# Windowed attention in a hybrid encoder layer: keys and values of a key head split once for all tokens, scaling by the sum on VectorE, two query buffers

## The chip, the core and the metric

The kernel runs on one core of a Trainium2 chip. The core has a matrix engine (TensorE, "PE" in the profile, with its weight loads shown apart as "PEld"), a vector engine (VectorE, "DVE"), a scalar engine (ScalarE, "ACT"), GpSimd ("POOL"), and SyncE ("SP"), which issues nearly all transfers of this kernel. Each engine works through its own queue of instructions in order and waits on semaphores for the others. The metric is device time in microseconds (us); lower is better.

## What is computed

One layer of an encoder for 1024 tokens of width 1024, in float32. It has four parts with RMS norms around them: a mixer with two branches that run side by side, (A) windowed attention and (B) a gated DeltaNet in both directions; one output projection of both; cross-attention into 256 memory tokens; and a SwiGLU feed-forward layer. The change touches branch (A). Eight query heads of width 64 share two key heads, four each, and a block of 128 queries sees its own block of keys and the two beside it. A learned "sink" logit takes part in the sum of the softmax. Cut to this branch:

```python
def _window_attention(q, k, v, sink):
    ...
    kw, vw = band(k), band(v)
    scores = jnp.einsum('bnqhgd,bnkhd->bnhgqk', qb, kw) * (ATTN_HEAD_DIM ** -0.5)
    ...
    scores = jnp.where(mask[None, :, None, None], scores, -jnp.inf)
    sk = sink.astype(jnp.float32).reshape(ATTN_KV_HEADS, ATTN_GROUP)[None, None, :, :, None, None]
    m = jnp.maximum(jnp.max(scores, axis=-1, keepdims=True), sk)
    p = jnp.exp(scores - m)
    denom = jnp.sum(p, axis=-1, keepdims=True) + jnp.exp(sk - m)
    o = jnp.einsum('bnhgqk,bnkhd->bnqhgd', p / denom, vw)
    return o.reshape(b, s, ATTN_WIDTH)
```

## The kernel before

Matrix products of float32 data are done on operands split in two: a high part, which is the value rounded to the type float32r by a copy on ScalarE, and a low part, which is the value less the high part, by a subtraction on VectorE or GpSimd. Three products (high by high, high by low, low by high) are added in PSUM. The helper `split` (lines 99 to 106) does this, and `load_w` (118 to 129) loads a slab of weights of 512 KB into one of two `wraw` buffers and splits it into `whi` and `wlo`.

The mixer is written as three lists of steps, which `issue` (687 to 690) runs in order. `ORDER_1` has the projections and preparation of the DeltaNet (`D`, `P`, `B`). `ORDER_2`, "G0 G1 G2 G3 L0 L1 V A4 A0 A1 W L2 L3 W W A2 A3 W", has the gate projections (`G`), the later levels of the DeltaNet's block inverses (`L`), the projections of values (`V`), keys (`A4`) and queries (`A0` to `A3`), and calls of `next_windows` (`W`). `ORDER_3` begins with `M`, the norm of the memory tokens, then five times "s01 W K", then further `s01` and `K`, and eight `K` at its end. `s01` is one of eight steps of the DeltaNet's scan for both head groups, a recurrence of small matrix products (line 763) with VectorE and ScalarE steps between them. `K` (`next_kv`, 883 to 902) is one of sixteen projections of the memory tokens for the cross-attention: 24 matmuls (891), a copy on ScalarE (893), a transfer, and for the last eight a transpose and a second copy (899, 901).

The program is put in order when it is built: a scheduler takes the instructions of each engine by priority, in general the order in which they are written, but puts a later one ahead where it is ready sooner by its own estimate. So windows, scan steps and projections are interleaved on every engine, and what stands later in the lists can run earlier.

Queries, keys and values go through DRAM: `attn_proj` (701 to 716) writes rotated queries and keys to `d_q` and `d_k` (head dimension by tokens), `value_proj` (718 to 729) writes `d_v` (token blocks by token by head dimension).

A window is one block of 128 queries with one key head: 8 blocks by 2 key heads, 16 windows. `window(n, g)` (598 to 666) is a generator in two halves. The first loads keys of the two or three blocks in sight twice, to both halves of the partitions (610), the block's queries of four heads likewise (611), and values (613). Keys and values are split here, for this window alone: `khi` on ScalarE (616), `klo` on GpSimd (617), `vhi` (621) and `vlo` (622), values doubled so that the product puts each head on both halves of the partitions. Queries hold the high part on partitions 0 to 63 and the low part on 64 to 127 (624, 625), so one matmul with 128 rows adds both. The raw keys, queries and values have one buffer each. Scores of a head are two matmuls (633) into a bank `pw` of PSUM; VectorE adds the band mask, scales, and takes the maximum (635); ScalarE takes the exponential with its sum (642); the sink's term comes in on four columns (645 to 647), the reciprocal on VectorE (648), and ScalarE multiplies each head's row by it (650). After the `yield` come, for each block of keys, four transposes into a `pw` bank (656), its split (659: cast on ScalarE, subtraction on VectorE) and three matmuls with the values as weights into `pow` (661). Two copies (664, 665) bring the even and the odd heads to the two halves of the partitions, and a transfer (666) writes them to `d_mix`.

`next_windows` (668 to 677) starts two windows a call and lets the second half of each window come after the first half of the next. After the scan, `d_mix` is read back (1023) and split, the output projection runs (`mid_gemm`, 967 to 1006), and the memory keys and values are read back and split (1033 to 1036).

Of the kernel before, what the change touches and what calls it, by code (L numbers as in the profile page):

```python
# [10 lines left out]
F32 = mybir.dt.float32  # L11
F32R = mybir.dt.float32r
I32 = mybir.dt.int32
AF = mybir.ActivationFunctionType
ALU = mybir.AluOpType
# [4 lines left out]
P = 128  # L20
S = 1024
D = 1024
KT = D // P
NT = S // P
HALF = 512
# [50 lines left out]
def tile_hybrid_block(  # L76
# [6 lines left out]
    nc = tc.nc  # L83
# [9 lines left out]
    def f32(ap):  # L93
        return ap.bitcast(F32)

    def bc(ap, axis, shape):
        return ap.unsqueeze(axis).to_broadcast(list(shape))
# [10 lines left out]
    def pool(name, bufs, **kw):  # L108
        return tc.tile_pool(name=name, bufs=bufs, reuse_waits="tile", **kw)
# [64 lines left out]
    d_k = dram.tile([P, S], F32, name="d_k")  # L174
    d_v = dram.tile([NT, P, P], F32, name="d_v")
# [346 lines left out]
    def levels(h):  # L522
# [72 lines left out]

        together([part(b) for b in range(2)])

    def window(n, g):

        tok = slice(n * P, (n + 1) * P)  # L600
# [1 line left out]
        nb = k1 - k0  # L602
        w = nb * P
        band = C[:, _AT["band0"] - C0 + (k0 - n + 1) * P:][:, 0:w]


        kr = tw.tile([P, 384], F32, tag="kr", name="kr", bufs=1)[:, 0:w]
        qr = tw.tile([P, 4, P], F32, tag="qr", name="qr", bufs=1)
        for r in range(2):
            nc.sync.dma_start(kr[64 * r:64 * r + 64], d_k[64 * g:64 * g + 64, k0 * P:k1 * P])  # L610
            nc.sync.dma_start(qr[64 * r:64 * r + 64], d_q[256 * g:256 * g + 256, tok].rearrange("(h e) t -> e h t", h=4))
        vr = tw.tile([P, 3, 64], F32, tag="vr", name="vr", bufs=1)[:, 0:nb]
        nc.sync.dma_start(vr, d_v[k0:k1, :, 64 * g:64 * g + 64].rearrange("c p e -> p c e"))
        khi = tw.tile([P, 384], F32R, tag="khi", name="khi")[:, 0:w]
        klo = tw.tile([P, 384], F32R, tag="klo", name="klo", bufs=1)[:, 0:w]
        nc.scalar.copy(khi, kr)
        nc.gpsimd.tensor_tensor(klo, kr, f32(khi), ALU.subtract)
        vhi = tw.tile([P, 3, 2, 64], F32R, tag="vhi", name="vhi")[:, 0:nb]
        vlo = tw.tile([P, 3, 2, 64], F32R, tag="vlo", name="vlo")[:, 0:nb]
        v2 = bc(vr, 2, (P, nb, 2, 64))  # L620
        nc.scalar.copy(vhi, v2)
        nc.gpsimd.tensor_tensor(vlo, v2, f32(vhi), ALU.subtract)
        qs = tw.tile([P, 4, P], F32R, tag="qs", name="qs")
        nc.scalar.copy(qs, qr)
        nc.gpsimd.tensor_tensor(qs[64:128], qr[64:128], f32(qs[64:128]), ALU.subtract)
# [4 lines left out]
        for hh in range(4):  # L630
            pp = pw.tile([P, 512], F32, tag="pw", name="psw")
            for i, kk in enumerate((khi, klo)):
                nc.tensor.matmul(pp[:, 0:w], qs[:, hh, :], kk, start=(i == 0), stop=(i == 1))
            sc = tw.tile([P, 384], F32, tag="sc", name="sc", bufs=8)
            nc.vector.tensor_tensor_reduce(out=sc[:, 0:w], in0=pp[:, 0:w], in1=band, scale=0.125,
                                           scalar=sink[:, 4 * g + hh:4 * g + hh + 1], op0=ALU.add, op1=ALU.max,
                                           accum_out=m4[:, hh:hh + 1])
            pr.append(sc)
# [8 lines left out]
        nc.vector.tensor_tensor(es, es, ssum, ALU.add)  # L647
        nc.vector.reciprocal(es, es)
        for hh in range(4):
            nc.scalar.mul(pr[hh][:, 0:w], pr[hh][:, 0:w], es[:, hh:hh + 1])  # L650
        yield
        po = pw.tile([P, 4, P], F32, tag="pow", name="pow", bufs=1)
        for j in range(nb):
            pp = pw.tile([P, 512], F32, tag="pw", name="ptw")
            for hh in range(4):
                nc.tensor.transpose(pp[:, hh * P:(hh + 1) * P], pr[hh][:, j * P:(j + 1) * P], ident)
            ph = tw.tile([P, 512], F32R, tag="ph", name="ph")
            pl = tw.tile([P, 512], F32R, tag="pl", name="pl")
            split(ph, pl, pp)
            for i, (vv, pe_) in enumerate(((vhi, ph), (vhi, pl), (vlo, ph))):  # L660
                nc.tensor.matmul(po.rearrange("p h t -> p (h t)"), vv[:, j].rearrange("p r e -> p (r e)"), pe_,
                                 start=(j == 0 and i == 0), stop=(j == nb - 1 and i == 2))
        ao = tw.tile([P, 2, P], F32, tag="ao", name="ao", bufs=1)
        nc.scalar.copy(ao[0:64], po[0:64, 0:4:2, :])
        nc.scalar.copy(ao[64:128], po[64:128, 1:4:2, :])
        nc.sync.dma_start(d_mix[g * 256:(g + 1) * 256, tok].rearrange("(k p) t -> p k t", p=P), ao)

    def next_windows():

        for _ in range(2):  # L670
            last = wins[-1] if wins else None
            if wins_done[0] < 2 * NT:
                wins.append(window(wins_done[0] % NT, wins_done[0] // NT))
                next(wins[-1])
            wins_done[0] += 1
            if last:
                next(last, None)

    wins, wins_done = [], [0]
    kqv = {0: kqv0}  # L680
# [15 lines left out]
    pw = p12.enter_context(pool("pw", 2, space=PSUM, side="right"))  # L696
    ps = pgs.enter_context(pool("psl", 2, space=PSUM))
    tw = p12.enter_context(pool("tw", 2))
    tl_ = p1.enter_context(pool("tl", 2))

    def attn_proj(ct):
# [669 lines left out]
```

## Time and profile before

| what | value |
|---|---|
| median of 3 runs | 1644.9 us (1640.13 to 1646.33) |
| the profiled execution: time, span | 1638.65 us, 1636.9 us |
| mean granted TensorE clock | 0.984 |
| ACT: scaling of rows, line 650 | 64 instructions, 32.5 us |
| ACT: split of keys and values, lines 616 and 621 | 32 instructions, 15.5 us |
| POOL: split of keys and values, lines 617 and 622 | 32 instructions, 31.1 us |
| VectorE: mask and maximum, line 635 | 64 instructions, 36.3 us |

The profile is of one execution. A row of a group reads: line, engine, operation, tile written <- tiles read, shapes, count | busy us in all, mean ns of one | idle time of the engine just before them and what ended it. In the table of stages a row is a stretch of the span, its length, the busy time (and count) of each engine in it, the granted TensorE clock, the share of time that the 16 DMA engines were busy, and GB/s. In the timeline a row is start, length, engine, line, operation and tiles; "x4" are four instructions merged, and brackets give the engine's idle time before and what ended it. "SPq" is SyncE issuing a transfer; the length is the time of the issue, not of the transfer.

### The profile page before, as it was taken

The page shows a single profiled execution, that of the slowest core. Times are in us where ns is not written, and L with a number is a line of the kernel's source. Part 1 is how long each engine was busy: PE and PEld are TensorE (multiplying, and loading weights), DVE is VectorE, ACT ScalarE, POOL GpSimd, SP SyncE. Part 2 cuts the span into 40 slices and gives each one's busy share as a digit, 9 for nine tenths or more (in the row PEclk, how much of TensorE's full clock was granted, in tenths as well). Part 3 has the DMA queues.
Part 4 walks back from the last instruction along what each step waited for, and adds up shares of the span by engine and source line. Part 5 has one row for each costly group of instructions (what it writes and reads, how often), then busy time and mean ns, then how long its engine had stood idle before and what let it go on. Part 6 is the DMA issues. An engine that isn't in the chain of part 4 may idle for free.

```text
span 1636.9 us, 21688 instructions
## 1 busy us (share of the span) xinstructions
PE 1556.8 (95%) x7802; PEld 1305.8 (80%) x7802; DVE 948.6 (58%) x1431; ACT 753.1 (46%) x1530; POOL 547.6 (33%) x501
## 2 busy tenths in 40 slices
PE   6999889998899979999999999999999999999998
PEld 5878778777799877788888777788888888888886
DVE  6855986966678844444346458776555553334332
ACT  6556552236758773554335565233333232444211
POOL 2467552334337500253202221343433441221100
PEclk9999999997999999999999999999999999999999
DMA  6134257574999583454213164442222223565452
GB/s 200 41 116 130 64 167 207 155 176 125 323 315 294 151 288 110 153 182 146 73 65 116 52 217 151 122 135 78 77 91 92 82 84 111 204 213 184 140 173 75
DMA packets 275560, 240.49 MB, mean 147 GB/s; under 512 B 43240, under 2 KB 226941, under 8 KB 275453
## 3 DMA queue, kind: packets, MB, share of 16 engines
q1 hardware_dynamic: 275453, 239.11, 47.0%
q8 instruction: 61, 1.00, 0.2%
q14 instruction: 46, 0.38, 0.1%
HBM read 177.69 MB, written 58.75 MB: 144 GB/s over the span
## 4 chain that ended last, share of the span: by engine, by line
PE 56%; DVE 2%; ACT 1%; issue 1%; DMA 1%; POOL 0%; SPq 0%; POOLq 0%; ACTq 0%; DVEq 0%
PE pmg L984 9%; PE pd L1325 7%; PE pd L1301 7%; PE pD L1155 7%; PE pE L1155 7%; PE pA L1155 6%; PE pcq L260 5%; PE pB L1155 3%; PE pcs L1064 1%; PE pco L1090 1%; DMA wraw<-in_w_gate_up_dram 1%; DVE wlo L103 0%; PE ptn L953 0%; PE pct L1080 0%; ACT xr L1001 0%
## 5 line engine op out<-in xcount | busy, mean ns | idle before, releaser
L102 ACT CAST whi<-wraw 128x1024 fp32r<-128x1024 f32 x108 | 113.1, 1049 | 163.8 <-issue 60.7
L103 POOL TENSOR_TENSOR wlo<-wraw,whi 128x1024 fp32r<-128x1024 f32 x48 | 118.3, 2465 | 173.3 <-ACT whi L102 157.0
L260 PE MATMUL pg<-hhi,whi 128*128 128x512 f32 x352 | 141.0, 402 | 0.0
L260 PE MATMUL pg<-hhi,wlo 128*128 128x512 f32 x352 | 140.3, 399 | 0.0
L260 PE MATMUL pg<-hlo,whi 128*128 128x512 f32 x352 | 140.0, 398 | 0.0
L103 DVE TENSOR_TENSOR wlo<-wraw,whi 128x1024 fp32r<-128x1024 f32 x60 | 74.5, 1244 | 87.5 <-ACT whi L102 83.4
L984 PE MATMUL pmg<-whi,b 128*128 128x512 f32 x384 | 117.7, 396 | 2.9 <-ACT whi L102 2.7
L1155 PE MATMUL pA<-b,whi 128*128 128x512 f32 x352 | 109.5, 392 | 1.3 <-ACT m L1172 1.3
L285 DVE SCALAR_TENSOR_TENSOR acc<-cp,cols,acc 128x1024 f32<-128x1024 f32 x48 | 75.8, 1580 | 34.2 <-ACT acc L283 33.6
L984 PEld LDWEIGHTS pmg<-whi,b 128*128 128x128 f32 x384 | 72.0, 190 | 18.6 <-ACT whi L102 3.5
L1232 POOL TENSOR_TENSOR act<-act,up 128x512 f32<-128x512 f32 x33 | 48.4, 1468 | 108.0 <-issue 58.4
L260 PEld LDWEIGHTS pg<-hhi,wlo 128*128 128x128 f32 x352 | 67.3, 191 | 13.4
L260 PEld LDWEIGHTS pg<-hhi,whi 128*128 128x128 f32 x352 | 67.3, 192 | 13.1 <-ACT hhi L102 0.3
L260 PEld LDWEIGHTS pg<-hlo,whi 128*128 128x128 f32 x352 | 67.1, 191 | 13.1
L1155 PEld LDWEIGHTS pA<-b,whi 128*128 128x128 f32 x352 | 65.3, 188 | 15.0 <-ACT m L1172 2.0
L984 PE MATMUL pmg<-wlo,b 128*128 128x512 f32 x192 | 71.6, 394 | 0.4 <-DVE wlo L103 0.4
L1155 PE MATMUL pA<-b,wlo 128*128 128x512 f32 x176 | 68.7, 391 | 1.0 <-DVE wlo L103 1.0
L1325 PE MATMUL pd<-wdh,ath 128*128 128x512 f32 x176 | 69.5, 395 | 0.0
L1325 PE MATMUL pd<-wdh,atl 128*128 128x512 f32 x176 | 69.4, 395 | 0.0
L1325 PE MATMUL pd<-wdl,ath 128*128 128x512 f32 x176 | 69.4, 395 | 0.0
L1301 PE MATMUL pd<-dl,whi 128*128 128x512 f32 x176 | 68.5, 389 | 0.0
L1301 PE MATMUL pd<-dh,wlo 128*128 128x512 f32 x176 | 68.3, 389 | 0.0
(390 smaller groups left out, 4189.6 us busy)
## 6 DMA issues: line engine op xcount, KB each, us to landing
wraw<-in_w_gate_up_dram SPq DMA_DIRECT2D x52, 512.0 KB, 4.2
kv<-d_kv SPq DMA_DIRECT2D x32, 512.0 KB, 6.5
wraw<-in_w_in_dram SPq DMA_DIRECT2D x22, 512.0 KB, 4.0
araw<-d_act SPq DMA_DIRECT2D x22, 512.0 KB, 3.3
draw<-in_w_down_dram SPq DMA_DIRECT2D x22, 512.0 KB, 4.1
atr<-d_act SPq DMA_DIRECT2D x16, 704.0 KB, 4.7
d_act<-act SPq DMA_DIRECT2D x40, 256.0 KB, 2.8
d_kv<-kv SPq DMA_DIRECT2D x8, 1024.0 KB, 6.4
```

What stands on the lines that cost most here:

```text
L102: nc.scalar.copy(hi, src)
L103: (eng or nc.vector).tensor_tensor(lo, src, f32(hi), ALU.subtract)
L260: nc.tensor.matmul(p_, w[:, k, :], ah[a][:, k, :], start=(k == 0 and i == 0), stop=(k == nk - 1 and i == 2))
L285: nc.vector.scalar_tensor_tensor(acc, cp[:, t:t + S], taps[t], acc, ALU.mult, ALU.add)
L984: nc.tensor.matmul(pp[t], act[a][:, k, tt], w_[:, kk, :], start=(k == 0 and i == 0), stop=(k == KT - 1 and i == 2))
L1064: nc.tensor.matmul(pp[:, t2_, :], q[a][:, ct, tt], kr_[b_][:, ct, :], start=(j == 0 and i == 0), stop=(j == 1 and i == 2))
L1090: nc.tensor.matmul(po, vr_[a][:, kt, cs], pts[kt][b_], start=(kt == 0 and i == 0), stop=(kt == 1 and i == 2))
L1155: nc.tensor.matmul(out_, w[a][:, k, :], xx[b_][:, k, :], start=(start and k == 0 and i == 0), stop=(k == HK - 1 and i == 2), skip_group_ch ...
L1232: nc.gpsimd.tensor_tensor(o_, o_, up, ALU.mult)
L1301: nc.tensor.matmul(pps[t], a[:, tt], b_, start=(f == 0 and i == 0), stop=(f == NF - 1 and i == 2))
L1325: nc.tensor.matmul(pp, a[:, f - f0], b_[:, f], start=(f == 0 and i == 0), stop=(f == NF - 1 and i == 2))
```

## The change

Keys and values of a key head are loaded and split once, by halves of 512 tokens, in a new function `window_keys(g, hf)`; windows read slices of the tiles `khi`, `klo`, `vhi` and `vlo`, which hold all 1024 tokens of one key head. The values aren't doubled any more, so the product fills partitions 0 to 63, and the second copy to `ao` reads these and writes partitions 64 to 127. The second key head takes the place of the first in the same tiles: its first half is written after the first half of window 6 has been issued, its second half after that of window 8 (the first of the second key head). The scaling by the reciprocal of the sum goes from ScalarE to VectorE. Raw keys, values and queries share one tag, `wr`, with two buffers.

```diff
@@ -595,6 +595,19 @@
 
         together([part(b) for b in range(2)])
 
+    def window_keys(g, hf):
+
+        ts, cs = slice(hf * HALF, (hf + 1) * HALF), slice(4 * hf, 4 * hf + 4)
+        kr = tw.tile([P, HALF], F32, tag="wr", name="kr")
+        for r in range(2):
+            nc.sync.dma_start(kr[64 * r:64 * r + 64], d_k[64 * g:64 * g + 64, ts])
+        nc.scalar.copy(khi[:, ts], kr)
+        nc.gpsimd.tensor_tensor(klo[:, ts], kr, f32(khi[:, ts]), ALU.subtract)
+        vr = tw.tile([P, HALF], F32, tag="wr", name="vr")[:, 0:256].rearrange("p (c e) -> p c e", c=4)
+        nc.sync.dma_start(vr, d_v[cs, :, 64 * g:64 * g + 64].rearrange("c p e -> p c e"))
+        nc.scalar.copy(vhi[:, cs], vr)
+        nc.gpsimd.tensor_tensor(vlo[:, cs], vr, f32(vhi[:, cs]), ALU.subtract)
+
     def window(n, g):
 
         tok = slice(n * P, (n + 1) * P)
@@ -602,24 +615,11 @@
         nb = k1 - k0
         w = nb * P
         band = C[:, _AT["band0"] - C0 + (k0 - n + 1) * P:][:, 0:w]
-
-
-        kr = tw.tile([P, 384], F32, tag="kr", name="kr", bufs=1)[:, 0:w]
-        qr = tw.tile([P, 4, P], F32, tag="qr", name="qr", bufs=1)
+        ks = slice(k0 * P, k1 * P)
+
+        qr = tw.tile([P, 4, P], F32, tag="wr", name="qr")
         for r in range(2):
-            nc.sync.dma_start(kr[64 * r:64 * r + 64], d_k[64 * g:64 * g + 64, k0 * P:k1 * P])
             nc.sync.dma_start(qr[64 * r:64 * r + 64], d_q[256 * g:256 * g + 256, tok].rearrange("(h e) t -> e h t", h=4))
-        vr = tw.tile([P, 3, 64], F32, tag="vr", name="vr", bufs=1)[:, 0:nb]
-        nc.sync.dma_start(vr, d_v[k0:k1, :, 64 * g:64 * g + 64].rearrange("c p e -> p c e"))
-        khi = tw.tile([P, 384], F32R, tag="khi", name="khi")[:, 0:w]
-        klo = tw.tile([P, 384], F32R, tag="klo", name="klo", bufs=1)[:, 0:w]
-        nc.scalar.copy(khi, kr)
-        nc.gpsimd.tensor_tensor(klo, kr, f32(khi), ALU.subtract)
-        vhi = tw.tile([P, 3, 2, 64], F32R, tag="vhi", name="vhi")[:, 0:nb]
-        vlo = tw.tile([P, 3, 2, 64], F32R, tag="vlo", name="vlo")[:, 0:nb]
-        v2 = bc(vr, 2, (P, nb, 2, 64))
-        nc.scalar.copy(vhi, v2)
-        nc.gpsimd.tensor_tensor(vlo, v2, f32(vhi), ALU.subtract)
         qs = tw.tile([P, 4, P], F32R, tag="qs", name="qs")
         nc.scalar.copy(qs, qr)
         nc.gpsimd.tensor_tensor(qs[64:128], qr[64:128], f32(qs[64:128]), ALU.subtract)
@@ -630,7 +630,7 @@
         for hh in range(4):
             pp = pw.tile([P, 512], F32, tag="pw", name="psw")
             for i, kk in enumerate((khi, klo)):
-                nc.tensor.matmul(pp[:, 0:w], qs[:, hh, :], kk, start=(i == 0), stop=(i == 1))
+                nc.tensor.matmul(pp[:, 0:w], qs[:, hh, :], kk[:, ks], start=(i == 0), stop=(i == 1))
             sc = tw.tile([P, 384], F32, tag="sc", name="sc", bufs=8)
             nc.vector.tensor_tensor_reduce(out=sc[:, 0:w], in0=pp[:, 0:w], in1=band, scale=0.125,
                                            scalar=sink[:, 4 * g + hh:4 * g + hh + 1], op0=ALU.add, op1=ALU.max,
@@ -647,9 +647,9 @@
         nc.vector.tensor_tensor(es, es, ssum, ALU.add)
         nc.vector.reciprocal(es, es)
         for hh in range(4):
-            nc.scalar.mul(pr[hh][:, 0:w], pr[hh][:, 0:w], es[:, hh:hh + 1])
+            nc.vector.tensor_scalar(pr[hh][:, 0:w], pr[hh][:, 0:w], es[:, hh:hh + 1], None, ALU.mult)
         yield
-        po = pw.tile([P, 4, P], F32, tag="pow", name="pow", bufs=1)
+        po = pw.tile([P, 4, P], F32, tag="pow", name="pow", bufs=1)[0:64]
         for j in range(nb):
             pp = pw.tile([P, 512], F32, tag="pw", name="ptw")
             for hh in range(4):
@@ -658,23 +658,29 @@
             pl = tw.tile([P, 512], F32R, tag="pl", name="pl")
             split(ph, pl, pp)
             for i, (vv, pe_) in enumerate(((vhi, ph), (vhi, pl), (vlo, ph))):
-                nc.tensor.matmul(po.rearrange("p h t -> p (h t)"), vv[:, j].rearrange("p r e -> p (r e)"), pe_,
+                nc.tensor.matmul(po.rearrange("p h t -> p (h t)"), vv[:, k0 + j], pe_,
                                  start=(j == 0 and i == 0), stop=(j == nb - 1 and i == 2))
         ao = tw.tile([P, 2, P], F32, tag="ao", name="ao", bufs=1)
-        nc.scalar.copy(ao[0:64], po[0:64, 0:4:2, :])
-        nc.scalar.copy(ao[64:128], po[64:128, 1:4:2, :])
+        for r in range(2):
+            nc.scalar.copy(ao[64 * r:64 * r + 64], po[:, r:4:2, :])
         nc.sync.dma_start(d_mix[g * 256:(g + 1) * 256, tok].rearrange("(k p) t -> p k t", p=P), ao)
 
     def next_windows():
 
         for _ in range(2):
             last = wins[-1] if wins else None
-            if wins_done[0] < 2 * NT:
-                wins.append(window(wins_done[0] % NT, wins_done[0] // NT))
+            n = wins_done[0]
+            if n < 2 * NT:
+                for hf in range(2) if n == 0 else ():
+                    window_keys(0, hf)
+                wins.append(window(n % NT, n // NT))
                 next(wins[-1])
             wins_done[0] += 1
             if last:
                 next(last, None)
+
+            if n in (NT - 2, NT):
+                window_keys(1, n == NT)
 
     wins, wins_done = [], [0]
     kqv = {0: kqv0}
@@ -696,6 +702,9 @@
     pw = p12.enter_context(pool("pw", 2, space=PSUM, side="right"))
     ps = pgs.enter_context(pool("psl", 2, space=PSUM))
     tw = p12.enter_context(pool("tw", 2))
+
+    khi, klo = (tw.tile([P, S], F32R, tag=t, name=t, bufs=1) for t in ("khi", "klo"))
+    vhi, vlo = (tw.tile([P, NT, 64], F32R, tag=t, name=t, bufs=1) for t in ("vhi", "vlo"))
     tl_ = p1.enter_context(pool("tl", 2))
 
     def attn_proj(ct):
```

## Prediction

> **What bounds the kernel now.** I read the page first: busy times per engine.
>
> ```profile
> PE 1556.8 (95%) x7802; PEld 1305.8 (80%) x7802; DVE 948.6 (58%) x1431; ACT 753.1 (46%) x1530; POOL 547.6 (33%) x501
> ```
>
> PE is the bound on the whole, so an edit that takes no matmul away can only fill holes in PE. Next, the table of stages, cut where the local attention starts and ends: stretch, its length, busy us (count) of PE, PEld, DVE, ACT and POOL, granted clock, DMA share, GB/s.
>
> ```profile
> 352.00:416.00 64.00, 53.59 (x266) 45.34 (x266) 39.08 (x96) 42.34 (x113) 27.45 (x28) 0.81 0.48 142
> 416.00:470.00 54.00, 52.03 (x395) 49.31 (x396) 37.40 (x103) 38.88 (x94) 20.55 (x18) 0.97 1.01 320
> 470.00:520.00 50.00, 47.97 (x383) 46.00 (x382) 40.86 (x112) 36.16 (x103) 27.75 (x29) 1.00 0.98 301
> 520.00:565.00 45.00, 42.80 (x323) 39.83 (x322) 36.34 (x90) 36.72 (x118) 28.94 (x35) 1.00 0.64 186
> 565.00:600.00 35.00, 31.41 (x220) 28.73 (x219) 18.01 (x38) 27.53 (x65) 3.38 (x6) 0.96 0.92 296
> 600.00:633.00 33.00, 24.79 (x125) 21.49 (x124) 18.07 (x14) 17.81 (x21) 0.00 (x0) 0.89 0.53 165
> ```
>
> Three stages follow. Before the scan (352 to 416) PE idles 64 - 53.6 = 10.4 us, at a granted clock of 0.81. In the scan (416 to 565) it idles 149 - 142.8 = 6.2 us of 149: PE is full, and the DMA engines nearly so up to 520. In the tail (565 to 633), with the last windows and memory projections, PE idles 68 - 56.2 = 11.8 us. What can be filled is 10.4 + 6.2 + 11.8 = 28.4 us; a PE without holes might also get its full clock back, at most 53.6 x 0.19 = 10 us in the first stage and 31.4 x 0.04 + 24.8 x 0.11 = 4 in the tail. Last, the waits between 290 and 633: who waits, for what, total, times, longest.
>
> ```profile
> POOL vlo L622 <- ACT vhi L621: 52.1, 8, 22.1
> ACT khi L616 <- DMA kr<-d_k: 18.5, 8, 4.3
> ...
> ACT qs L624 <- DMA qr<-d_q: 13.5, 4, 8.6
> ```
>
> ```profile
> PE pow L661 <- ACT ph L102: 4.6, 5, 1.3
> ```
>
> ACT stands still 32.0 us behind loads of keys and queries, and POOL 52.1 us behind a cast of values; whatever is queued behind them on these engines waits too. PE itself waits only 4.6 us for a window's cast.
>
> **The change, part by part.** These groups leave or move (count, total us, mean ns):
>
> ```profile
> L650 ACT ACTIVATE sc<-sc,es 128x384 f32<-128x384 f32 (+1 forms) x64 | 32.5, 585 | 1.2 <-DVE es L648 1.1
> ...
> L622 POOL TENSOR_TENSOR vlo<-vr,vhi 128x384 fp32r<-128x384 f32 (+1 forms) x16 | 16.1, 1009 | 86.8 <-ACT vhi L621 52.1 <-PE psw L633 17.2 <-PE ptw L656 12.1
> ...
> L617 POOL TENSOR_TENSOR klo<-kr,khi 128x384 fp32r<-128x384 f32 (+1 forms) x16 | 15.0, 940 | 17.0 <-PE psw L633 12.8 <-ACT khi L616 3.7 <-issue 0.5
> ...
> L616 ACT CAST khi<-kr 128x384 fp32r<-128x384 f32 (+1 forms) x16 | 7.8, 485 | 18.5 <-DMA kr<-d_k 18.5
> L621 ACT CAST vhi<-vr 128x384 fp32r<-128x384 f32 (+1 forms) x16 | 7.7, 484 | 12.9 <-PE pow L661 8.2 <-DMA vr<-d_v 4.7
> ```
>
> *Splits.* ACT loses 7.8 + 7.7, POOL 15.0 + 16.1. Four calls of window_keys come in their place, with keys 512 wide and values 256 wide. The nearest row of that width:
>
> ```profile
> L102 ACT CAST ph<-ptw 128x512 fp32r<-128x512 f32 x44 | 25.5, 584 | 7.2 <-PE ptw L656 7.0
> ```
>
> A key cast costs 0.58 us, a value cast at half that width at most as much. POOL's 940 ns stand for 384 columns mostly, so a key half costs between that and 512 / 384 of 1009 = 1.35 us, and values 256 wide less than the 1.0 of their row; I take 1.33 and 0.8. So ACT gains at most 4 x 1.16 = 4.6 and POOL 4 x 2.1 = 8.5. Net: ACT -11, POOL -22.6.
>
> *Scaling.* ACT loses another 32.5, in all 32.5 + 11 = 43 us. DVE gets 64 products from SBUF to SBUF with one scalar per partition. The same operation stands in the trace at two other widths:
>
> ```profile
> L869 DVE TENSOR_SCALAR mt<-mt,mrs x2: 743/748/754, 411.5 to 413.5; 128x1024 f32<-128x1024 f32 x2
> ```
>
> ```profile
> L640 DVE TENSOR_SCALAR nm<-m x16: 157/170/659, 365.5 to 584.9; 128x4 f32<-128x4 f32 x16
> ```
>
> That makes (748 - 170) / 1020 = 0.567 ns a column: 385 ns at 384 columns (48 times), 313 at 256 (16 times), 23.5 us in all. The other end is the pass over a bank of scores at this width, 612 ns, so 64 x 0.61 = 39 us at most; I take 23.5, since it is the same instruction.
>
> ```profile
> L635 DVE CUSTOM_DVE_ANT_0 sc<-psw,C,prm 128x384 f32<-128x384 f32 x48 | 28.8, 612 | 17.9 <-PE psw L633 17.6
> ```
>
> *Transfers.* SP issued 32 key and 16 value loads (min/median/max ns):
>
> ```profile
> L610 SPq DMA_DIRECT2D kr<-d_k x32: 473/588/3772, 312.9 to 558.3; - x32
> ```
>
> ```profile
> L613 SPq DMA_DIRECT2D vr<-d_v x16: 359/392/691, 292.5 to 568.8; - x16
> ```
>
> It now issues 8 and 4: 24 x 0.588 + 12 x 0.392 = 18.8 us less in SP's queue, which also carries the scan's loads and the weights.
>
> *At nothing.* The half-width weights of the last product: PE's pace there is set by 512 moving columns, and a weight load overlaps. The copy of the odd heads from partitions 0-63 to 64-127: no row shows a crossing copy; I take it as long as its neighbour, and at twice that it would add under 6 us to ACT, which loses 43. The second head's split has to wait for readers of the first: the halves are replaced two windows after their last use, and if that cover failed the cast would hold up ACT, with the scan's copies and the windows' exponentials queued behind it, and one window would be late by a load, a cast and a subtraction (4.3, the longest wait above, + 0.58 + 1.33 = 6.2 us), once or twice, under a PE that is full with the scan. A query load can now wait for a split, since they share two buffers: the same 6.2 us in the same place. The first head's split is free: its keys are there at 312.9, the first load of the row above, 39 us ahead of the windows.
>
> **The sum.** *Before the scan*: the scan starts when its first loads land, and they stand behind a window's loads on SP.
>
> ```profile
> 405.69 0.36 SPq L594 DMA_DIRECT2D d_pz<-Z  x1
> 406.15 0.46 SPq L613 DMA_DIRECT2D vr<-d_v  x1
> 406.70 1.82 SPq L610 DMA_DIRECT2D kr<-d_k  x2
> ...
> 409.98 0.54 SPq L771 DMA_DIRECT2D kv<-d_kv  x1
> ```
>
> ```profile
> 416.26 1.08 PE L763 MATMUL psc<-kv,pz 128*128 128x128 f32 x4 [2.67 <-DMA pz<-d_pz]
> ```
>
> Value and key issues there (0.46 + 1.82 = 2.3 us) go. I take -2.5 with some of ACT's relief; the ends are -10.4 (all idle) and +1.5 (four products, 4 x 0.385, in front of the last Z on DVE). *Scan*: of 6.2 us of idle PE I take -2, under half of the 4.6 us that PE waits for casts; the ends are -6.2 and the rival's +14.6 below. *Tail*: a projection ends with its copy on ACT.
>
> ```profile
> 571.45 0.37 ACT L893 COPY cv<-pck 128x256 f32<-128x256 f32 x1
> ...
> 591.07 0.37 ACT L893 COPY cv<-pck 128x256 f32<-128x256 f32 x1 [0.83 <-PE pck L891]
> ...
> 618.90 0.37 ACT L893 COPY cv<-pck 128x256 f32<-128x256 f32 x1
> ```
>
> Four took 19.6 us to 591.07, the last three 27.8, while ACT was 27.53 of 35 us busy. The products on ACT, by stage:
>
> ```profile
> 416.00:470.00 54.00, 6.45 (x12) 0.97 1.01 320
> 470.00:520.00 50.00, 6.05 (x13) 1.00 0.98 301
> 520.00:565.00 45.00, 6.15 (x13) 1.00 0.64 186
> 565.00:600.00 35.00, 5.76 (x12) 0.96 0.92 296
> ```
>
> In the last stage these 5.8 us, plus a value cast or two (0.5 each), leave ACT: -6.5, if ACT is what the projections wait for; the ends are -11.8 and 0. Sum: -2.5 - 2 - 6.5 = -11, against the profiled execution's 1638.65 (span 1636.9 and 1.75 around it): 1627.7. The median of the runs, 1644.9, is 6.25 above that execution, so in the runs I expect 1634.
>
> **Rivals.**
>
> *PE is full anyway.* Windows that end sooner bring their matmuls from the tail into the scan; the last products alone:
>
> ```profile
> 565.00:600.00 35.00, 8.97 (x27) 4.63 (x27) 0.96 0.92 296
> ```
>
> These 9 us of busy PE meet a scan with 6.2 to spare, which then ends between 3 and 9 later, some 6, and that eats the tail's 6.5: -2.5 - 2 + 0, so 1634 in the profile's terms, 1640 in the runs. For: PE idles only 4% of the scan. Against: the 10.4 us ahead of it can take windows too.
>
> *DVE becomes the scan's bound (slower).* In the scan DVE is busier than ACT already: 114.6 of 149 us against 111.8. The products of this stage (12 + 13 + 13 = 38) add 38 x 0.385 = 14.6: 129 of 149, 87%. Each window puts a block of 1.54 us into the queue on which the scan's recurrence has its own serial steps. If each block delays the recurrence by its length, the scan ends 14.6 later, and the tail, a row of projections after the scan, keeps its length: -2.5 + 14.6 = +12, so 1651, in the runs 1657. It decides where the blocks fall between a scan matmul and the DVE step it waits for. Against: DVE had 34 us free there, over twice the added work.
>
> *DVE and POOL in each other's way.* The same two sums on DVE, alone and beside a POOL instruction:
>
> ```profile
> 554.94 0.75 DVE L831 TENSOR_TENSOR ol<-ol,of 128x256 f32<-128x256 f32 x2
> ...
> 558.01 1.85 DVE L831 TENSOR_TENSOR ol<-ol,of 128x256 f32<-128x256 f32 x2
> ```
>
> ```profile
> 558.08 1.50 POOL L625 TENSOR_TENSOR qs<-qr,qs 64x512 fp32r<-64x512 f32 x1
> ```
>
> 1.1 us were lost. If each of some 9.5 blocks in the scan meets one, 9.5 x 1.1 = 10.5 us late; with the 11 gained that is no change, 1644. Against: POOL loses 22.6 us of work, so there is less to meet. The Trainium skill, "SBUF — State Buffer", section "Who interferes with whom", says that a VectorE `tensor_scalar` in a two-port mode and a GpSimd instruction lock each other out of a shared port pair for a whole instruction. By that rule the moved products, unlike ScalarE's, can be locked out; the pair of rows above agrees for two-input sums, and no row here shows it for a wide product.
>
> *More than I take.* All 28.4 us of idle PE filled: 1610, in the runs 1616; with the clock's 14 us as well, 1602. For: 84 us of waits at the head of ACT's and POOL's queues. Against: the levels before the scan and the projections behind it are chains of their own.
>
> **How the numbers follow.** Forecast 0.42, more than that 0.08, PE full 0.16, DVE against POOL 0.06, DVE the bound 0.28. About 0.5% (8.2 us) is what a measurement tells from no change, so faster 0.50, same 0.22, slower 0.28. The time is the likeliest's, 1634; its own range, with the tail's and the scan's bounds, is 1622 to 1639. With cases of both signs the range goes from 1613, past all idle filled, to 1658, just past the slower rival.
>
> **What would show it.** The products on VectorE at 0.39 us; 8 key and 4 value loads; ACT some 43 us less busy, POOL 22 less, DVE 23 more; the scan's first matmul before 416, and the last projection's copy some 11 us before 618.9. It is wrong if the scan (first to last of its matmuls) takes longer than 149 us, with waits of the scan's matmuls for DVE, or if the tail keeps its length with ACT free: then loads or the projections' own chain set it.

## The result and the profile after

The changed kernel is slower: 1647.07 us median of 20 runs (1643.7 to 1654.03), the kernel before 1640.34 on the same chip (20 runs, 1635.16 to 1646.64). The ratio is 1.0043, with a 95% interval of 1.0033 to 1.0053. The forecast was 1634 us, and a gain: the sign was wrong. 1647 lies outside the 1622 to 1639 us that went with the forecast itself, and inside the whole range of 1613 to 1658 that also covered the rivals. The profiled execution took 1651.6 us (span 1649.9), which is 4.5 above its median, while that of before (1638.65) lies 1.7 below its own: the two traces differ by 13.0 us, the medians by 6.7.

First the page's line of busy times, then the table of stages with the columns of before:

```profile
PE 1556.3 (94%) x7802; PEld 1300.9 (79%) x7802; DVE 968.8 (59%) x1495; ACT 714.2 (43%) x1442; POOL 526.5 (32%) x477
```

```profile
352.00:416.00 64.00, 50.58 (x272) 42.45 (x272) 41.17 (x105) 31.43 (x89) 20.69 (x22) 0.89 0.48 140
416.00:470.00 54.00, 47.98 (x357) 43.86 (x357) 37.99 (x110) 29.56 (x70) 15.82 (x12) 0.98 1.05 322
470.00:520.00 50.00, 47.50 (x382) 45.13 (x381) 42.23 (x119) 25.10 (x75) 21.11 (x21) 1.00 0.79 260
520.00:565.00 45.00, 43.05 (x335) 39.77 (x334) 40.77 (x107) 28.40 (x101) 23.86 (x31) 1.00 0.61 177
565.00:600.00 35.00, 30.83 (x210) 27.25 (x208) 20.77 (x48) 19.79 (x47) 2.80 (x4) 0.95 0.87 282
600.00:633.00 33.00, 19.55 (x117) 16.06 (x117) 18.25 (x27) 22.60 (x39) 0.20 (x1) 0.80 0.61 187
```

The work went where the diff sends it: ACT has 38.9 us less, POOL 21.1 less, VectorE 20.2 more, and TensorE the same. But TensorE was less busy in these stages: 189.1 us from 352 to 565 where it had 196.4, and 50.4 from 565 to 633 where it had 56.2. These 7.3 and 5.8 us are the 13 by which the traces differ. Behind that nothing of weight differs: the matmul of the output projection that stood at 636.50 us stands at 649.86, 13.4 later, and the end comes 13.0 later. Busy time is not work where the clock differs: ahead of the scan TensorE is 3.0 us less busy and yet has six matmuls more on record (272 and 266), at a granted clock of 0.89 instead of 0.81. So part of the 7.3 is a faster clock.

The second loss has one place. The projections of the memory tokens, whose last copy on ACT stood at 618.90, end no later now. It is the windows that do: their last write to `d_mix`, and the first matmul of the output projection, stood in the timeline of before at

```profile
599.27 0.36 SPq L666 DMA_DIRECT2D d_mix<-ao  x1
```

```profile
619.51 0.71 PE L984 MATMUL pmg<-whi,b 128*128 128x512 f32 x2
```

and stand now, on ACT, on SP and on TensorE, at

```profile
617.34 0.36 ACT L902 COPY cv<-pck 128x256 f32<-128x256 f32 x1
...
620.49 0.74 ACT L665 COPY ao<-pow 64x256 f32<-64x256 f32 x2 [1.26 <-PE pow L661]
...
623.06 4.83 ACT L102 CAST b<-mraw 128x1024 fp32r<-128x1024 f32 x5
...
630.12 2.23 ACT L102 CAST b<-mraw 128x1024 fp32r<-128x1024 f32 x2
```

```profile
621.25 0.36 SPq L666 DMA_DIRECT2D d_mix<-ao  x1
623.28 0.36 SPq L1044 DMA_DIRECT2D mvr<-d_mv  x1
623.73 1.86 SPq L1032 DMA_DIRECT2D mraw<-d_mix  x3
```

```profile
631.21 2.08 PE L993 MATMUL pmg<-whi,b 128*128 128x512 f32 x4 [10.81 <-ACT b L102]
```

Before, the last write came 19.6 us ahead of the last copy; now it comes 3.9 behind it. Behind the write come three loads of mixed rows (five others were issued at 573 us), a flight of 7.1 us, and a cast. Before, all that lay under the last projections; now TensorE stands 10.8 us for it. The five casts at 623.06 are rows that were there; the two at 630.12 are those it waits for.

### The profile page after: what moved, and what is told of

It reads as the page before. It is cut to its first block, busy times and chain, and to the rows that moved or that the text cites. A ratio compares the mean times of both kernels' runs of the same rounds, so it can differ in the third digit from the quotient of the medians.

```text
span 1649.9 us, 21541 instructions
## 1 busy us (share of the span) xinstructions
PE 1556.3 (94%) x7802; PEld 1300.9 (79%) x7802; DVE 968.8 (59%) x1495; ACT 714.2 (43%) x1442; POOL 526.5 (32%) x477
## 4 chain that ended last, share of the span: by engine, by line
PE 64%; DVE 10%; DMA 7%; ACT 4%; issue 3%; SPq 2%; POOL 1%; POOLq 0%; ACTq 0%; DVEq 0%
PE pmg L993 10%; PE pd L1334 7%; PE pd L1310 7%; PE pE L1164 7%; PE pD L1164 7%; PE pA L1164 6%; PE pcq L260 5%; PE pB L1164 3%; PE psc L772 3%; DMA wraw<-in_w_ckv_dram 2%; PE pck L900 2%; PE pcs L1073 1%; DVE acc L285 1%; PE pco L1099 1%; DVE A L512 1%
## 5 line engine op out<-in xcount | busy, mean ns | idle before, releaser
L260 PEld LDWEIGHTS pg<-hhi,whi 128*128 128x128 f32 x352 | 67.0, 191 | 13.4 <-ACT hhi L102 0.6
```

The lines of the kernel that those rows point to most:

```text
L260: nc.tensor.matmul(p_, w[:, k, :], ah[a][:, k, :], start=(k == 0 and i == 0), stop=(k == nk - 1 and i == 2))
```

## Experiments

Each is a kernel with the diff shown, compared with the kernel before on the same chip. "Write" is the last window's write to `d_mix`, "copy" the last projection's copy on ACT, "start" the first matmul of the output projection. Each of these times is read from one execution.

**The two halves of the change, each by itself.** The scaling back on ScalarE in the changed kernel (`a_actmul`), and the scaling on VectorE in the kernel before (`b_dvemul`):

```diff
-            nc.vector.tensor_scalar(pr[hh][:, 0:w], pr[hh][:, 0:w], es[:, hh:hh + 1], None, ALU.mult)
+            nc.scalar.mul(pr[hh][:, 0:w], pr[hh][:, 0:w], es[:, hh:hh + 1])
```

> The changed kernel with the 64 scaling products back on ScalarE; the split once and the shared buffers stay. Theory S (the scaling on VectorE makes each window's own chain longer, so that the last window's output is written about 22 us later, at 621 instead of 599 us, and the output projection waits for its read-back): the write returns to 599 to 608 us, the output projection starts at full pace before 626 us, and the time is 1636 to 1641 us. Rival B (the split once does it: a load of queries waits for a buffer that raw keys and values share, and the first queries come 7.6 us later): the write stays behind 614 us and the time at 1645 to 1649 us.

> The kernel before with one edit: the 64 scaling products go to VectorE; keys and values are split in each window as before, with their own buffers. Theory S: the last window's output is written behind 614 us and the time is 1645 to 1652 us, a ratio of 1.003 to 1.007 to the kernel before. Rival B: without the shared buffers nothing is lost, the write stays at 599 to 604 us and the time at 1638 to 1642 us. If the products on VectorE hindered GpSimd (or the reverse), a product would take well over the 0.39 us that the forecast took, and GpSimd's own subtractions would be longer than in the kernel before.

Measured: 1.0003 (0.9988 to 1.0018) and 1.0016 (1.0001 to 1.0032), where the whole change has 1.0043. From the first trace the issues of line 666 (min/median/max ns, first and last start), the last copy and the start:

```profile
L666 SPq DMA_DIRECT2D d_mix<-ao x16: 359/374/3886, 397.5 to 612.0; - x16
```

```profile
624.09 0.37 ACT L902 COPY cv<-pck 128x256 f32<-128x256 f32 x1
```

```profile
624.70 0.71 PE L993 MATMUL pmg<-whi,b 128*128 128x512 f32 x2
```

From the second the last write and the start:

```profile
612.41 0.37 SPq L666 DMA_DIRECT2D d_mix<-ao  x1
```

```profile
621.25 0.80 PE L984 MATMUL pmg<-whi,b 128*128 128x512 f32 x1 [1.79 <-ACT b L102]
```

Both expectations for the write failed in part: each edit alone moves it by some 13 us (599.3 to 612.0 and to 612.4), both by 22. In time, one costs nothing and the other little. The two sum to 0.19%, with some 0.2% of uncertainty, which lies just clear of the 0.43% of both. That is a slack used up, though not in the same way in each. Before, 10.0 us behind the write (the distance in the trace of after) was 609.3, and TensorE came free at 619.5: 10.2 us were to spare. With the products on VectorE alone, 13 exceed them by little: the start waits 1.79 us for a cast. With the split alone the start doesn't wait for the write at all: it is 0.6 behind the copy, which itself comes 5.2 us later than before (624.1), and the rest of the span is 3.0 us shorter (1014.4 and 1017.4). Twenty-two exceed them by much. Theory S had the time of the first kernel and rival B that of the second; neither is the whole.

**Buffers.** Raw keys and values move into the buffers of the scores, so that queries have two of their own; with the products on VectorE (`a_scraw`) and on ScalarE (`a_scraw_actmul`):

```diff
+        for q in range(2):
+            ts = slice(hf * HALF + 256 * q, hf * HALF + 256 * (q + 1))
+            kr = tw.tile([P, 384], F32, tag="sc", name="kr", bufs=8)[:, 0:256]
...
+        vr = tw.tile([P, 384], F32, tag="sc", name="vr", bufs=8)[:, 0:256].rearrange("p (c e) -> p c e", c=4)
```

> The changed kernel, its raw keys and values in the eight buffers of the scores (keys in four pieces instead of two), so that the two query buffers hold queries alone; the scaling stays on VectorE. Theory S: 1644 to 1649 us, the last write behind 612 us. Rival B: 1638 to 1642 us, the last write at 599 to 604 us.

> Both edits: raw keys and values in the buffers of the scores, and the scaling back on ScalarE. What is left of the change is the split once, with two query buffers: ScalarE and GpSimd have only less to do. Theory S and rival B both expect the last write at or before 604 us; then the end is that of the last K projections (their copies ended at 619 us before), 1634 to 1640 us. If it is 1645 us or more, neither the scaling nor the shared buffers is the cause, and another order of the instructions is.

Measured: 1.0093 (1.0075 to 1.0112), with copy and write at 623.0 and 626.9, and 0.9985 (0.9971 to 0.9999), with 620.9 and 608.8 (604 was expected; the time is as expected). The shared buffers aren't the cause: taking them apart makes the first slower still, more than either theory had it, which stays unexplained. With the buffers apart, the split once is worth 0.15% where the scaling stays on ScalarE and the projections set the start.

**The handover itself.** Only the first call of `mid_gemm` takes the pieces of the contraction in another order, the scan's half first; all windows stay as they are. In the changed kernel (`a_korder`) and in the kernel before (`b_korder`):

```diff
-            for kp in range(4):
+            for kp in kps:
...
-    xn0 = mid_gemm(tz, mxT[0], w_out, gp, x, d_x1, 0)
+    xn0 = mid_gemm(tz, mxT[0], w_out, gp, x, d_x1, 0, kps=(2, 3, 0, 1))
```

> The changed kernel, windows and all as they are; only the first call of the output projection takes its four pieces of the contraction in the order 2, 3, 0, 1, so that it begins with the scan's half of the mixed rows (loaded back at 572 us, long before) and comes to the windows' half later. Theory H (the loss is made at this handover alone: the windows end at 621 us, their half is loaded back and cast until 631 us, and nothing is left to cover it): the first matmul of the output projection comes at 623 to 626 us instead of 631.2, although the last window still ends at 621 us, and the time is 1637 to 1643 us. Rival G (the slower windows cost along the way, in scan and projections, and the wait at the end only shows it): no gain of more than 2 us, 1645 to 1649 us.

> The kernel before with the same edit of the order. By theory H nothing is to be had here, since the windows' half lands and is cast by 612 us and the projection waits for TensorE, which is at the last K projections until 619.5 us: 1638 to 1642 us, a ratio of 0.998 to 1.001. If the order were a gain by itself, it would be below 0.997 here too.

Measured: 1.0016 (1.0006 to 1.0027) and 1.0027 (1.001 to 1.0043). In the first, on SP, on ACT and on TensorE:

```profile
616.34 0.36 SPq L666 DMA_DIRECT2D d_mix<-ao  x1
```

```profile
616.34 1.90 ACT L102 CAST kr<-mkr 128x2048 fp32r<-128x2048 f32 x1
618.14 4.83 ACT L102 CAST b<-mraw 128x1024 fp32r<-128x1024 f32 x5
```

```profile
619.24 2.07 PE L993 MATMUL pmg<-whi,b 128*128 128x512 f32 x4 [3.74 <-ACT b L102]
```

TensorE starts 2.9 us behind the write instead of 10.0, and of the 0.43% lost 0.27 come back, 4.4 us, with every window as it was: the greater part of the loss is made at this handover. The 2.9 that are left are not for the write's rows: the start waits for the first cast of rows that were loaded long before, and in ACT's queue this cast stands behind the last window's copies and a cast of the memory keys. Write and copy both came 4.9 us earlier than in the trace of after, though all engines have the same instructions in the same order ahead of the handover, and the write is 3.9 behind the copy in both. So where the pair lies varies from one execution to the next by about 5 us, more than many of the distances between kernels here, and the distance of write and copy belongs to the program. Of the 7.3 us of the scan's stages half is that one execution's: TensorE is busy 192.8 us there in this trace, and 189.1 in that of after. In the kernel before the edit gains nothing, as theory H has it, but it costs 0.27% where nothing was expected; its profiled execution starts at 620.5 and shows no reason. That is left open, and with it whether the 4.4 us are all that the wait cost.

**The late first window.** The first load of queries is written ahead of the keys' loads and splits; the rest as in the changed kernel (`a_qfirst`), and with the scaling on ScalarE (`a_actmul_qfirst`):

```diff
-                for hf in range(2) if n == 0 else ():
-                    window_keys(0, hf)
                 wins.append(window(n % NT, n // NT))
...
+        for hf in range(2) if (n, g) == (0, 0) else ():
+            window_keys(0, hf)
         qs = tw.tile([P, 4, P], F32R, tag="qs", name="qs")
```

> The changed kernel; only the first window's load of queries is written ahead of the four loads and four splits of keys and values, instead of behind them. Theory D (two delays add up at the end: the first score comes 7.6 us late because of what stands ahead of it, and the scaling on VectorE adds some 10 us more): the first score returns to 354 to 357 us, the last window's output to 610 to 616 us, and the time to 1639 to 1644 us. If the first window's start does not matter for the end, the last write stays at 619 to 623 us and the time at 1645 to 1649 us.

> The same, with the scaling back on ScalarE: neither delay. Theory D: the last write at 598 to 606 us, so that the last K projections set the end again as in the kernel before; 1635 to 1640 us, a ratio of 0.996 to 1.000. If the split once had a cost of its own beside the late start, the write stays at 610 us or later.

Measured: 1.0017 (1.0004 to 1.003), first score at 358.4, write at 615.3; and 1.0043 (1.003 to 1.0055), write at 618.8, copy at 624.8. The first has the write and the time of theory D, though its first score came 1.4 us later than expected, and the same windows without the edit wrote at 616.3 in the execution of `a_korder`. The second is a plain miss: with an early first window the last one came later. Two windows on, nothing of the early start is left in either: the third window's first score comes 0.8 and 1.2 us later than without the edit. The delays aren't terms that can be added; each edit gives the scheduler another order of the whole stretch.

**Other engines for the products.** GpSimd in VectorE's place (`a_poolmul`), the last two heads of four on ScalarE (`a_half`, shown), and GpSimd with the early queries (`a_poolmul_qf`):

```diff
-            nc.vector.tensor_scalar(pr[hh][:, 0:w], pr[hh][:, 0:w], es[:, hh:hh + 1], None, ALU.mult)
+            (nc.vector.tensor_scalar(pr[hh][:, 0:w], pr[hh][:, 0:w], es[:, hh:hh + 1], None, ALU.mult) if hh < 2
+             else nc.scalar.mul(pr[hh][:, 0:w], pr[hh][:, 0:w], es[:, hh:hh + 1]))
```

> The changed kernel with the 64 scaling products on GpSimd, which is busy for 61 of the 149 us of the scan, where VectorE has 121. By the nearest row (GpSimd's subtraction of 128x384, 1.0 us in the kernel before) four products take 4 us of a window's chain there, against 1.7 us on VectorE and 2.4 on ScalarE. Theory Q (the windows end late because their steps queue on the fullest engine): with the products on the emptiest one the last window's output is written by 612 us, the output projection starts by 625 us, and the time is 1636 to 1642 us. Rival L (what counts is the length of a window's own chain): the write stays at 621 us or later and the time at 1647 us or more.

> The changed kernel with the products of two heads of four on VectorE and two on ScalarE. Theory Q: half of what VectorE was given goes back, so the last write lies between the two (612 us with all on ScalarE, 621 us with all on VectorE): 614 to 619 us; with the 9 to 10 us from there to the first matmul of the output projection and 1017 us from that to the end, 1640 to 1645 us. If the lag comes by steps (a window takes its place in TensorE's order after one projection more or less), the write may lie as late as 622 us with the time at 1646 to 1648 us.

> Products on GpSimd and the first window's load of queries ahead of the keys. Two of the edits that brought the last write forward together: write at 598 to 606 us. From there on the last K projections set the start of the output projection (they ended at 619 us in the kernel before), so no more than 1635 to 1639 us, a ratio of 0.996 to 1.000. If the write comes behind 612 us, the early load of queries costs as much as it did with the products on ScalarE (write at 619 us, 1645 us).

Measured: 1.0089 (1.0062 to 1.0117), 1.0002 (0.9985 to 1.0019) and 1.007 (1.0044 to 1.0097). With GpSimd, the group of the products, and write, copy and start:

```profile
L650 POOL TENSOR_SCALAR sc<-sc,es 128x384 f32<-128x384 f32 x48 | 59.2, 1250 | 25.5 <-DVE es L648 21.5 <-ACT mjk L875 3.8
```

```profile
612.60 0.36 SPq L666 DMA_DIRECT2D d_mix<-ao  x1
```

```profile
632.25 0.36 ACT L902 COPY cv<-pck 128x256 f32<-128x256 f32 x1
```

```profile
632.86 0.71 PE L993 MATMUL pmg<-whi,b 128*128 128x512 f32 x2
```

2.7 times VectorE's price for a product (1250 ns against 455), and the write still comes at 612.6, on the edge of theory Q's expectation; with the early queries it comes at 598.7. So the length of a window's own chain isn't what makes it late (rival L). But the time is no better, because now the projections are late: their copy comes at 632.3 and 629.3, and the start is 0.6 behind it. Windows and projections share TensorE and ACT, and what is put ahead for one may be taken from the other: 8 of the 16 projections start ahead of the last window's first score, where 13 did in the trace of after. That this is the reason is argued, not shown; TensorE also waits 12.5 us for casts of the windows' transposed rows (`ph`) here, and 6.1 in after. With half the products on each engine the write comes at 610.3 (614 to 619 was expected), and the copy already at 606.4. TensorE is busy 142.7 of the scan's 149 us there, as it was before (142.8); with all products on VectorE it was 138.5.

**Half the products and the other order, together** (`a_half_k`): the order of pieces of `a_korder`, and two heads on each engine, here every other head instead of the first two and the last two:

```diff
-            nc.vector.tensor_scalar(pr[hh][:, 0:w], pr[hh][:, 0:w], es[:, hh:hh + 1], None, ALU.mult)
+            if hh % 2:
+                nc.scalar.mul(pr[hh][:, 0:w], pr[hh][:, 0:w], es[:, hh:hh + 1])
+            else:
+                nc.vector.tensor_scalar(pr[hh][:, 0:w], pr[hh][:, 0:w], es[:, hh:hh + 1], None, ALU.mult)
...
-    xn0 = mid_gemm(tz, mxT[0], w_out, gp, x, d_x1, 0)
+    xn0 = mid_gemm(tz, mxT[0], w_out, gp, x, d_x1, 0, kps=(2, 3, 0, 1))
```

> Two edits that did well by themselves: the products of two heads on VectorE and of two on ScalarE, and the first call of the output projection beginning with the scan's half of the rows. Theory M (the output projection starts at the later of two times: 0.6 us behind the last K projection's copy, and 9 to 10 us behind the last window's write, or 3 us behind it where it begins with the scan's half; the end comes 1017 us later, within 3): the copy at 606 us and the write at 610 us of the run with half the products allow a start at 613 us, so 612 to 617 us and a time of 1631 to 1637 us, a ratio of 0.995 to 0.999. If what is saved there is lost again (the same order of the pieces made the kernel before 0.1 to 0.4 % slower): 1638 to 1642 us.

Measured: 0.9966 (0.9949 to 0.9982), 1633.63 us beside 1638.5, and

```profile
603.01 0.37 ACT L905 COPY cv<-pck 128x256 f32<-128x256 f32 x1
```

```profile
606.93 0.36 SPq L669 DMA_DIRECT2D d_mix<-ao  x1
```

```profile
609.82 2.08 PE L996 MATMUL pmg<-whi,b 128*128 128x512 f32 x4 [3.74 <-ACT b L102]
```

Copy and write lie 3 us earlier than in the run with half the products alone, so the start of 609.8 is earlier than the 612 to 617 expected; time and ratio are as expected. No run tells whether every other head does that: the trace of `a_half` lies 1.6 us above its median and this one 2.8 below, which would be enough. The handover gains here as it did in `a_korder`: 2.9 us lie between write and start, where `a_half` has 9.9. This kernel is 0.34% faster than the kernel before, and faster than the changed one.

**One rule for all.** From each trace: copy, write, start, and from the start to the end of the span. The rule: the start is the later of copy + 0.6 and write + 9.3 (+ 2.9 with the scan's half first).

| kernel | ratio | copy | write | write - copy | start | by the rule | start to end |
|---|---|---|---|---|---|---|---|
| before | 1 | 618.9 | 599.3 | -19.6 | 619.5 | 619.5 | 1017.4 |
| after | 1.0043 | 617.3 | 621.3 | +3.9 | 631.2 | 630.6 | 1018.7 |
| a_actmul | 1.0003 | 624.1 | 612.0 | -12.1 | 624.7 | 624.7 | 1014.4 |
| b_dvemul | 1.0016 | 618.4 | 612.4 | -5.9 | 621.3 | 621.7 | 1019.3 |
| a_scraw | 1.0093 | 623.0 | 626.9 | +3.9 | 636.8 | 636.3 | 1019.0 |
| a_scraw_actmul | 0.9985 | 620.9 | 608.8 | -12.1 | 621.6 | 621.5 | 1014.8 |
| a_korder | 1.0016 | 612.4 | 616.3 | +3.9 | 619.2 | 619.2 | 1020.1 |
| b_korder | 1.0027 | 619.9 | 599.0 | -20.9 | 620.5 | 620.5 | 1017.5 |
| a_qfirst | 1.0017 | 614.2 | 615.3 | +1.1 | 623.8 | 624.6 | 1018.5 |
| a_actmul_qfirst | 1.0043 | 624.8 | 618.8 | -6.0 | 628.2 | 628.1 | 1018.1 |
| a_poolmul | 1.0089 | 632.3 | 612.6 | -19.7 | 632.9 | 632.9 | 1016.1 |
| a_half | 1.0002 | 606.4 | 610.3 | +3.9 | 620.2 | 619.6 | 1019.3 |
| a_poolmul_qf | 1.007 | 629.3 | 598.7 | -30.6 | 630.0 | 629.9 | 1016.3 |
| a_half_k | 0.9966 | 603.0 | 606.9 | +3.9 | 609.8 | 609.8 | 1019.3 |

The rule gives all fourteen starts within 0.9 us, and the rest of the span takes 1014 to 1020. The 0.6, 9.3 and 2.9 are read from these same traces; what tests them is that they hold over an edit of the handover alone, and that the last kernel was put together by them. The last column has two groups: 1014.4 to 1017.5 in the six kernels whose start is set by the copy, 1018.1 to 1020.1 in the eight where it is set by the write. Behind a start that had to wait, the rest took some 3 us more.

## Why the prediction was wrong

*The parts were priced well.* ACT was to lose 43 us and lost 38.9, POOL 22.6 and 21.1; VectorE was to gain 23.5 and gained 20.2. The groups of the new instructions:

```profile
L650 DVE TENSOR_SCALAR sc<-sc,es 128x384 f32<-128x384 f32 x48 | 18.8, 455 | 0.1
```

```profile
L605 POOL TENSOR_TENSOR klo<-kr,khi 128x512 fp32r<-128x512 f32 x4 | 5.1, 1282 | 8.8 <-ACT khi L604 8.8
...
L609 POOL TENSOR_TENSOR vlo<-vr,vhi 128x256 fp32r<-128x256 f32 x4 | 2.9, 734 | 8.4 <-ACT vhi L608 8.4
...
L604 ACT CAST khi<-kr 128x512 fp32r<-128x512 f32 x4 | 2.5, 620 | 10.6 <-DMA kr<-d_k 9.6 <-PE psw L633 0.9
```

A key subtraction was taken at 1.33 us and takes 1.28, a value subtraction 0.8 and 0.73, a key cast 0.58 and 0.62; products come out at 18.8 + 5.6 = 24.4 us against 23.5 (5.6 being the 16 at 256 columns); one takes 455 ns and not 385, but the four of a block overlap. The copy that crosses partitions, unpriced by any row, is no longer than its neighbour: the 32 copies of line 665, half of them crossing, took 362 to 368 ns with a median of 366, where the two lines had medians of 363 and 368. The 6.25 us between the profiled execution and the runs, which the sum added at its end, came from three runs; over twenty the distance is 1.7. And the ends -2.5 - 6.2 - 11.8 and -2.5 - 2 + 0 give 1624 to 1640 us, not the forecast's 1622 to 1639.

*Before the scan, -2.5:* its first matmul came at 414.68 instead of 416.26, -1.6. *Scan, -2:* from its first matmul to its last it took 138.6 us and takes 142.2, +3.6, with the error of one execution on it. The sign was wrong and the size small; the 149 us named as the mark were not reached.

*Tail, -6.5, with -11.8 and 0 for ends:* this is the step that failed. "A projection ends with its copy on ACT" is true, and the last copy did come 1.6 us sooner, where some 11 were forecast. But the term took these projections for the end of the stage. The output projection waits for the later of two things, and the other one, the windows' write, went by 22 us from 20 ahead of the copy to 4 behind it. In the prediction windows could only come sooner (the rival of a full TensorE rests on that). That they might come later, and that their read-back had cover of 10.2 us, was priced nowhere. The start moved by +11.7 in the traces; by the ratios of `a_korder` and after, 4.4 us of the 6.7 lost were this wait.

*"At nothing":* the half-width weights and the crossing copy were rightly put at nothing. The buffers shared by keys, values and queries were given 6.2 us "in the same place", under a TensorE full with the scan. The first score came 7.6 us late instead, ahead of the scan (columns as before; first and last start in the middle, before and after):

```profile
L633 PE MATMUL psw<-khi,qs x64: 274/339/667, 354.1 to 582.2; 128*128 128x384 f32 x48, 128*128 128x256 f32 x16
```

```profile
L633 PE MATMUL psw<-khi,qs x64: 278/339/522, 361.7 to 602.6; 128*128 128x384 f32 x48, 128*128 128x256 f32 x16
```

The shared buffers aren't the reason (`a_scraw` has its first score at 363.4). The first load of queries is issued at 350.99 us, at 347.82 before; `a_qfirst`, with the load ahead of the keys' work and issued at 350.71, brought 3.3 of the 7.6 us back, and the rest stays open. Whether that delay reached the end is not shown either: with the early first score the last write came at 615.3 in one run and at 618.8 in the other. What fails is the reasoning that a delay of the windows under a full TensorE is free: their last write is one side of a join.

*The rivals.* "VectorE becomes the scan's bound" had the sign, at a chance of 0.28, and not the place: the scan grew by 3.6 us and not by 14.6. The blocks of products were there, 1.40 us each (priced at 1.54). With the products on VectorE the last windows moved back: by their first matmuls in the trace, 13 of the 16 projections started ahead of the last window's first score, where 10 had; with the products alone on VectorE 12, with the split alone 10. But half the products also has 13, and its write comes 11 us sooner. Nor does VectorE's busy time put the writes in order: of the scan's 149 us it is busy 121.0 in after (write at 621.3), 120.6 with half the products (610.3), 124.6 in `b_dvemul` (612.4) and 109.1 with the split alone (612.0). So a full VectorE is not by itself what holds the windows, and why the two edits together hold them longest stays open.

## What to carry to other kernels

Before work is moved to another engine, look for the stage's last join and note for each branch that arrives there how early it is: an edit that delays the branch with slack shows nothing until the slack is gone, and then two edits that cost little or nothing can make one loss. Relief of an engine is worth nothing if the branch it serves isn't the one that arrives last, and a join can often be eased at the join itself, here by beginning with the operands that have long been there. Where a scheduler orders the whole, two edits don't add, so each is to be run alone and together.

## What the runs showed of the hardware

*A wide product waits out a GpSimd instruction.* Two blocks of four products of one shape in the trace of after, and the GpSimd instruction beside the first:

```profile
484.44 2.15 DVE L650 TENSOR_SCALAR sc<-sc,es 128x256 f32<-128x256 f32 x4
...
501.09 1.14 DVE L650 TENSOR_SCALAR sc<-sc,es 128x256 f32<-128x256 f32 x4
```

```profile
484.70 1.48 POOL L625 TENSOR_TENSOR qs<-qr,qs 64x512 fp32r<-64x512 f32 x1 [5.33 <-ACT qs L624]
```

The block lost 1.0 us. The prediction had no row for a wide product: the rule of the Trainium skill ("SBUF — State Buffer", "Who interferes with whom"), that a two-port VectorE instruction and a GpSimd one lock each other out, holds for it. Three of the sixteen blocks were hit so hard, some 2.6 us in all (1.0 here, 0.8 each for two of 384 columns), and two more lost 0.3 and 0.2; the rival had 10.5.

*The wait at the join costs clock too.* The output projection's first matmuls in the trace of after, and two stretches of its table of stages:

```profile
633.73 0.79 PE L993 MATMUL pmg<-whi,b 128*128 128x512 f32 x1 [0.44 <-DVE b L103]
...
636.03 0.63 PE L993 MATMUL pmg<-whi,b 128*128 128x512 f32 x1
...
637.37 0.39 PE L993 MATMUL pmg<-wlo,b 128*128 128x512 f32 x1
```

```profile
631.20:637.40 6.20, 5.75 (x14) 4.06 (x15) 6.11 (x6) 2.09 (x2) 0.00 (x0) 0.54 0.13 49
637.40:645.00 7.60, 7.60 (x35) 6.29 (x34) 3.36 (x3) 1.06 (x1) 0.00 (x0) 1.00 0.21 60
```

The granted clock is 0.54 for the first 6.2 us and 1.00 from 637.4 on; a matmul of 512 columns takes 0.63 us and then 0.39. Before, where TensorE had waited 1.3 us, it took 0.39 from 620.07 on. The Trainium skill ("TensorE: Matmul & The Clock Gate", "What's actually happening") says that an idle window of about 3.4 us halves the clock and a busy one restores it, and that these windows run on their own time; by that page the slow stretch would be an estimated 3.4 to 6.8 us. The trace agrees: its slow stretch is 6.2 us.
